# Four conv row blocks of an output projection as two pairs by Strassen's algorithm, with one written-out order for all engines, in a hybrid decoder layer

## The chip, the cores and the metric

The kernel runs on one core of a Trainium2 chip. The metric is the device time of one execution in microseconds; several executions are taken, and their median is given. Two kernels are compared on the same chip.

In the profile PE is the tensor engine, PEld its weight loads, DVE the vector engine, ACT the scalar engine, POOL the engine called GpSimd, and SP the engine that only issues transfers here. A row of a timeline reads: start, duration, engine, line, operation, output <- inputs, shape, count, and in brackets the idle time before it with what ended that.

## The reference

One layer with a conditioned mixer and a conditioned convolutional feed-forward part, for 512 tokens of 1024 channels. `ada_w` gives six modulation vectors from the condition `c`. What the change touches is the product with `w_out`, whose 2048 rows are 1024 of the mLSTM heads (`h`) and 1024 of the convolution group (`y`), and what follows it:

```python
mod = cond @ ada_w[l] + ada_b[l]
sh1, sc1, g1, sh2, sc2, g2 = jnp.split(mod[:, None, :], N_MOD, axis=-1)
...
mix = jnp.concatenate([h, y], axis=-1) @ w_out[l]
x = x + g1 * rms_norm(mix, mix_post_g[l])
u = rms_norm(x, ffn_pre_g[l]) * (1.0 + sc2) + sh2
up = causal_dwconv(u @ ffn_up[l], ffn_conv_w[l], ffn_conv_b[l])
```

All of it is float32.

## The kernel before

Every float32 product is made of three: each operand is split into a high part, rounded to the type `fp32r`, and a low part, the rest (`w_split` at L164 for weights, on ACT and POOL), and `mm3` (L186) issues high times high, high times low and low times high into one bank of PSUM, 128x512 float32.

The 512 tokens are four token tiles of 128. The 2048 rows of `w_out` are 16 blocks of 128, 0 to 7 from the heads and 8 to 15 from the convolution; `MIX` is the order in which they are used. The 1024 output columns are two halves of 512. `mixa` is the first half, four banks, one for each token tile; `mixb` is the second. `mix_first(n)` (L812 to L833) adds row block `MIX[n]` to the four banks of `mixa` with 12 matmuls. It stands between the steps of the last head's attention (`steps`), so that TensorE has work while the head's softmax and normalisation run. Then eight row blocks go into `mixb` (L847 to L851), all four token tiles after one another, and `mix_last(tt, a, b)` (L902) adds the other eight for one token tile at a time, so that a tile's row is whole early. `wo_rows` loads four row blocks of a half, 1 MB, by SP's queue into one of two buffers (`raws`) and splits them.

The modulation vectors are made beside this, by 48 sums, each of 1024 products for 128 outputs (`ada_block`, L147): a transfer of 0.5 MB by ACT's queue, then one VectorE instruction that multiplies and sums, L155. Sums 16 to 23 give `g1`; 24 to 39 give `sh2` and `sc2`. The latter were put behind the head's last split (`last_lo`). `ada_done` adds the bias, L160, and L852 to L854 turn the result into `gains`, which TensorE transposes (`gT` of 16 rows, L643, in `send_rows`); the rows go through DRAM (`row_d`) and come back spread over all partitions as `gs2r` and `sh2r` (`row`, L653). In the same way `gT` of 8 rows gives `g1r`.

For each token tile a chain follows when its `mixa` and `mixb` banks are whole: `sq_sum` on ACT (L668, `mixa0junk`, `mixb0junk`) sums the squares, `chain_sums` makes `un = mixb * g1r` and the factor `rm` (two small steps, DVE and POOL), `chain_x` the new `x1` and its sum of squares, with `gs2r`, `chain_u` the normalised input `un` with `sh2r`. TensorE transposes it (`xT`, L892), ACT and DVE split it (`u2h`, `u2l`), and `up`, the feed-forward product, begins. `mg` (L844) is `mixa * g1r`, made for four tiles while `mixb` is computed. `up_split` splits the second and third block of `w_up`, loaded by SP (L909).

What sets the order: on each engine instructions run in the order in which they were recorded and then scheduled by a planner that goes by priority; `with in_order()` keeps the recorded order for what stands in it, and `behind` pins one instruction after another of the same engine. Each engine's queue is in order, so an instruction that waits holds up all behind it. The queues of SP and ACT also issue transfers.

## Time and profile before

| | us |
|---|---|
| median of three runs | 773.16 |
| lowest and highest | 772.98, 774.11 |
| the profiled execution | 772.58 |
| its span in the profile | 770.9 |
| TensorE busy in it | 757.8 |
| VectorE busy | 606.3 |
| ScalarE busy | 403.9 |
| POOL busy | 350.9 |

The span is from the first to the last instruction in the profile; the execution's own time is 1.7 us longer. The mean granted TensorE clock was 0.997 of full speed.

The last head's attention and the first half of the projection lie at about 316 to 370 us, the first eight blocks of the second half at 370 to 392, the rest of it to 415, and from there `up` runs.

### The profile page before, as it was taken

To read this page: it belongs to the slowest core of one execution; us is meant where nothing else is said; L and a number is where in the kernel's file an instruction comes from. 1 tells how busy PE (TensorE), PEld (TensorE's weight loads), DVE (VectorE), ACT (ScalarE), POOL (GpSimd) and SP (SyncE) were. 2 spreads that over 40 slices of the span, in tenths; PEclk is the share of its full clock that TensorE was granted. 3 is DMA by queue.
4 is the path that set the end of the run, shared out by engine and by line. 5 is a ranking of instruction groups with operands and counts; after the bars stand their busy time and mean duration, and the time that the engine had idled before them with its cause. 6 is when DMAs were issued, how large, how long until landed. Compare 5 with 4: busy or idle time off the path is not lost.

```text
span 770.9 us, 10631 instructions
## 1 busy us (share of the span) xinstructions
PE 757.8 (98%) x3709; PEld 637.3 (83%) x3709; DVE 606.3 (79%) x967; ACT 403.9 (52%) x761; POOL 350.9 (46%) x286
## 2 busy tenths in 40 slices
PE   7999999999999999999999999999999999999996
PEld 5788898778888888988888998888888888878885
DVE  6987999999999856747758798666555687699996
ACT  5447256677676457572343554444444444455762
POOL 1029578697797645442751456444444440000001
PEclk9999999999999999999999999999999999999998
DMA  8983214204023552425953653333233321787872
GB/s 325 341 334 137 84 55 164 82 29 164 28 82 110 166 177 96 162 111 187 379 195 114 245 187 130 130 130 109 96 117 124 131 91 60 260 277 226 302 261 109
DMA packets 36409, 125.33 MB, mean 163 GB/s; under 512 B 4194, under 2 KB 5634, under 8 KB 30468
## 3 DMA queue, kind: packets, MB, share of 16 engines
q1 hardware_dynamic: 24372, 96.17, 35.5%
q10 hardware_dynamic: 11984, 28.48, 10.6%
q8 instruction: 29, 0.48, 0.2%
q14 instruction: 24, 0.20, 0.1%
HBM read 113.22 MB, written 11.42 MB: 162 GB/s over the span
## 4 chain that ended last, share of the span: by engine, by line
PE 90%; DVE 4%; DMA 2%; ACT 2%; issue 1%; POOL 0%; SPq 0%; DVEq 0%; ACTq 0%; POOLq 0%
PE up L190 10%; PE up L189 10%; PE up L188 10%; PE qko L188 6%; PE qko L189 5%; PE qko L190 5%; PE p L1175 5%; PE glu L189 3%; PE glu L188 3%; PE glu L190 3%; PE glu L316 2%; PE mixa L190 2%; PE mixa L188 2%; PE mixa L189 2%; PE mixb L188 2%; PE mixb L190 2%
## 5 line engine op out<-in xcount | busy, mean ns | idle before, releaser
L721 DVE SCALAR_TENSOR_TENSOR cv<-gt,cvw,cv 128x489 f32<-128x489 f32 (+23 forms) x200 | 136.9, 728 | 3.3 <-ACT cv L709 2.2
L675 POOL TENSOR_TENSOR ro2r<-ro2t,mhalf 128x1 f32<-128x1 f32 x1 | 0.5, 537 | 120.5 <-DVE ro2t L673 120.5
L171 POOL TENSOR_TENSOR wup_1024l<-wup,wup_1024h 128x512 fp32r<-128x512 f32 x20 | 27.5, 1373 | 31.7 <-ACT wup_1024h L170 31.6
L717 POOL TENSOR_TENSOR cs<-cs,cs 128x510 f32<-128x510 f32 (+3 forms) x32 | 41.3, 1291 | 0.2
L171 POOL TENSOR_TENSOR wup_0l<-wup,wup_0h 128x512 fp32r<-128x512 f32 x20 | 27.3, 1367 | 29.1 <-ACT wup_0h L170 29.1
L171 POOL TENSOR_TENSOR wup_1536l<-wup,wup_1536h 128x512 fp32r<-128x512 f32 x20 | 27.0, 1349 | 28.8 <-ACT wup_1536h L170 28.8
L155 DVE SCALAR_TENSOR_TENSOR junk<-ada,cb 128x1024 bf16<-128x1024 f32 x20 | 31.1, 1554 | 7.8 <-DMA ada<-in_adaT 7.7
L189 PE MATMUL up<-u2l,wup_0h 128*128 128x512 f32 (+1 forms) x100 | 36.5, 365 | 0.2 <-DVE u2l L900 0.2
L188 PE MATMUL up<-u2h,wup_0h 128*128 128x512 f32 (+1 forms) x100 | 36.5, 365 | 0.0
L188 PE MATMUL up<-u2h,wup_1024h 128*128 128x512 f32 (+1 forms) x100 | 36.4, 364 | 0.0
L190 PE MATMUL up<-u2h,wup_0l 128*128 128x512 f32 (+1 forms) x100 | 36.4, 364 | 0.0
L188 PE MATMUL up<-u2h,wup_512h 128*128 128x512 f32 (+1 forms) x100 | 36.4, 364 | 0.0
L189 PE MATMUL up<-u2l,wup_512h 128*128 128x512 f32 (+1 forms) x100 | 36.4, 364 | 0.0
L190 PE MATMUL up<-u2h,wup_512l 128*128 128x512 f32 (+1 forms) x100 | 36.4, 364 | 0.0
L188 PE MATMUL up<-u2h,wup_1536h 128*128 128x512 f32 (+1 forms) x100 | 36.4, 364 | 0.0
L189 PE MATMUL up<-u2l,wup_1536h 128*128 128x512 f32 (+1 forms) x100 | 36.4, 364 | 0.0
L190 PE MATMUL up<-u2h,wup_1536l 128*128 128x512 f32 (+1 forms) x100 | 36.4, 364 | 0.0
L190 PE MATMUL up<-u2h,wup_1024l 128*128 128x512 f32 (+1 forms) x100 | 36.4, 364 | 0.0
L189 PE MATMUL up<-u2l,wup_1024h 128*128 128x512 f32 (+1 forms) x100 | 36.3, 363 | 0.0
L171 POOL TENSOR_TENSOR wup_512l<-wup,wup_512h 128x512 fp32r<-128x512 f32 x20 | 27.7, 1383 | 14.9 <-ACT wup_512h L170 14.9
L715 ACT ACTIVATE cs<-gt,cvw 128x511 f32<-128x511 f32 (+4 forms) x40 | 27.4, 715 | 8.1 <-POOL cs L717 3.6
L170 ACT ACTIVATE wup_1024h<-wup 128x512 fp32r<-128x512 f32 x22 | 13.9, 631 | 25.1 <-PE up L189 21.4
(1070 smaller groups left out, 2663.6 us busy)
## 6 DMA issues: line engine op xcount, KB each, us to landing
wup<-in_w_up SPq DMA_DIRECT2D x22, 1024.0 KB, 6.6
wqko<-in_w_qko SPq DMA_DIRECT2D x12, 1024.0 KB, 4.8
ada<-in_adaT ACTq DMA_DIRECT2D x20, 512.0 KB, 4.3
ada<-in_adaT SPq DMA_DIRECT2D x16, 512.0 KB, 7.4
wo<-in_w_out SPq DMA_DIRECT2D x8, 1024.0 KB, 4.8
spare<-in_adaT ACTq DMA_DIRECT2D x12, 512.0 KB, 7.6
wd<-in_w_down SPq DMA_DIRECT2D x6, 768.0 KB, 6.5
g2kept<-g2d SPq DMA_DIRECT2D x11, 384.0 KB, 7.3
```

The lines of the kernel that those rows point to most:

```text
L155: t = V.scalar_tensor_tensor(out=junk, in0=r, scalar=1.0, in1=cb, op0=ALU.mult, op1=ALU.mult, accum_out=mod[:, i : i + 1])
L170: S.activation(hi[:, :n], src, AF.Copy)
L171: (eng or G).tensor_tensor(out=lo[:, :n], in0=src, in1=hi[:, :n].bitcast(F32), op=ALU.subtract)
L188: PE.matmul(ps, a[0], b[0], start=start, stop=False)
L189: PE.matmul(ps, a[0], b[1], start=False, stop=False)
L190: PE.matmul(ps, a[1], b[0], start=False, stop=stop)
L316: PE.matmul(banks0[i], blk(wk, i)[a], u[k][b], start=k == 0 and a == b, stop=False)
L675: G.tensor_tensor(out=r, in0=t, in1=mhalf[:, :1], op=ALU.pow)
L715: S.activation(t[:, d:], cvx[j][:, : T - d], AF.Copy, scale=w(CK - 1 - d))
L717: G.tensor_tensor(out=side[:, d:], in0=side[:, d:], in1=t[:, d:], op=ALU.add)
L721: last_tap[0] = V.scalar_tensor_tensor(out=cp[:, d:], in0=cvx[j][:, : T - d], scalar=w(CK - 1 - d), in1=cp[:, d:], op0=ALU.mult, op1=ALU.add)
L1175: PE.matmul(ps[q], x, y, start=False, stop=m == NM - 1 and i == 2, skip_group_check=True)
```

## The change

It takes the four convolution blocks 12 to 15 out of `MIX` and computes them as two pairs (12, 13) and (14, 15) by Strassen's algorithm: the two-by-two blocks are the two token halves (256 tokens), the two row blocks of the pair, and the two column halves. Seven products, p1 to p7, of two token tiles each take the place of eight; each is 6 matmuls for one pair, and the two pairs add up in the same banks. Strassen's sums over the tokens are made by `token_sums`, those over the weights by `row_sums` and `row_last`, in place in the loaded weights `wo_raw` (2 MB in the freed buffer of `u`, a new input `w_os` in which the host has set the four quarters of each pair side by side). `row_part` splits the weight sums with the low part on VectorE. The products use the banks of `mixa` and `mixb`: p1, p6, p7 in the banks of `mixb` 2 and 3, p5, p3 in 0 and 1, p2 in `mixa` 0 and 1, p4 in 2 and 3. Where a product belongs in several of the outputs, ACT copies the bank out (`op1`, `op5`, `ou`, `op7`) and VectorE adds the copy onto the other banks.

Half `mixb` now gets four row blocks for all tiles (`KA` = 4) and eight by `mix_last`. All of it stands in one `in_order()` block, for all engines. The loads of `x1` move from ACT's queue to SP's, behind the loads of `w_out`; the row `g1r` is sent and fetched by SP. Eleven of the sums 24 to 39 move up: 24 to 28 between the last head's projections, 29 to 34 ahead of the scaling of `hn`; 35 follows the splits for p4, 36 the first additions onto `mixa`, and 37 to 39 the last. Two small vectors, `cvw` and `ghalf`, are pinned behind the last split of `u`.

```diff
-MIX = [*range(6), *range(8, 14), 6, 7, 14, 15]
+MIX = [*range(6), *range(8, 12), 6, 7]
+PAIRS = [(12, 13), (14, 15)]
...
-    KA = 8
+    HT = T // 2
+    KF = 12
+    KA = 4
...
+    def token_sums(za, zb, name):
+        sums, s4 = cvtile(f"os{name}"), cvtile(f"o4{name}")
+        s1, s2 = sums[:, :HT], sums[:, HT:]
+        V.tensor_tensor(out=s1, in0=za[:, HT:], in1=zb[:, HT:], op=ALU.add)
+        V.tensor_tensor(out=za[:, HT:], in0=za[:, :HT], in1=za[:, HT:], op=ALU.subtract)
+        V.tensor_tensor(out=s2, in0=s1, in1=za[:, :HT], op=ALU.subtract)
+        V.tensor_tensor(out=s4[:, :HT], in0=zb[:, :HT], in1=s2, op=ALU.subtract)
+        return {"a": za, "b": zb, "s": sums, "4": s4[:, :HT]}
+    def token_part(z, kinds, name):
+        at = lambda z, h: [tuple(v[:, h * HT + q * P : h * HT + (q + 1) * P] for v in z) for q in range(2)]
+        out = {}
+        for n in kinds:
+            if n == "4":
+                t = slot(f"o4{name}t", F32R)
+                out["p3"] = at(pair(z[n], t[:, :HT], t[:, HT:]), 0)
+            else:
+                t = pair(z[n], slot(f"oh{name}{n}", F32R), slot(f"ol{name}{n}", F32R))
+                for h, which in enumerate({"a": ("p1", "p7"), "b": ("p2", "p4"), "s": ("p5", "p6")}[n]):
+                    out[which] = at(t, h)
+        return out
+    def row_part(which, m):
+        b = {"p1": 1, "p2": 0, "p6": 1, "p7": 2, "p3": 3, "p4": 0}.get(which)
+        z = ot1[m] if which == "p5" else wraw[m][:, b * T : (b + 1) * T]
+        wf[which, m] = w_split(z, f"o{which}_{m}", eng=V)
+    def row_sums(m):
+        b21, b11, b12, b22 = (wraw[m][:, b * T : (b + 1) * T] for b in range(4))
+        V.tensor_tensor(out=b12, in0=b22, in1=b12, op=ALU.subtract)
+        V.tensor_tensor(out=b11, in0=b11, in1=b12, op=ALU.add)
+    def row_last(m):
+        b21, b11 = (wraw[m][:, b * T : (b + 1) * T] for b in range(2))
+        V.tensor_tensor(out=b21, in0=b21, in1=b11, op=ALU.subtract)
+    def block(which, m):
+        ps = {"p1": banks[2:], "p6": banks[2:], "p7": banks[2:], "p5": banks[:2], "p3": banks[:2], "p2": mixa[:2], "p4": mixa[2:]}[which]
+        for q in range(2):
+            mm3(ps[q], tf[m][which][q], wf[which, m], m == 0 and which in ("p1", "p5"), m == 1, True)
...
+            if j >= KT // 2:
+                continue
...
+            tc.cur_priority += LATER
+            for i in range(16, 24):
+                ada_block(i, last_tap[0])
+            for i in range(24, 29):
+                ada_block(i, taps[H - 1, 1 if i < 27 else 3], acts[H - 1, 0 if i < 27 else 2])
+            tc.cur_priority -= LATER
...
         if h == H - 2:
             norm_sums()
-    tc.cur_priority += LATER
-    for i in range(16, 24):
-        ada_block(i, last_tap[0])
     ada_done(16, 24)
-    tc.cur_priority -= LATER
     gain(0, 16, "mix_post_g")
-    wo = {}
+    wo, tf, wf = {}, {}, {}
     steps = attention(H - 1)
     next(steps)
     mix_first(0)
+    wraw = upool.tile([P, 2, 2048], F32, tag="uh", name="wo_raw")
+    wraw = [wraw[:, m, :] for m in range(2)]
     next(steps)
     norm_rows()
-    mix_first(1)
-    mix_first(2)
-    mix_first(3)
-    mix_first(4)
+    za = token_sums(ys[4], ys[5], "0")
+    tf[0] = token_part(za, "asb4", "0")
+    spare.append(upool.tile([P, KT, T], F32, tag="ul", name="spare"))
+    for n in range(1, 5):
+        mix_first(n)
+    for m, r in enumerate(wraw):
+        nc.sync.dma_start(r, w_os[m])
+    rows0 = turn_rows(0, KT, cvbank)
     next(steps)
     mix_first(5)
     next(steps)
     mix_first(6)
-    next(steps)
-    for n in range(7, 10):
-        mix_first(n)
-    for _ in steps:
-        pass
-    spare.append(upool.tile([P, KT, T], F32, tag="ul", name="spare"))
-    for i in range(24, 40):
-        ada_block(i, last_lo[0])
+    mid = wo_rows(0, 8, 10)
+    ot1 = []
+    for m in range(2):
+        ot1.append(cvtile(f"ot1_{m}"))
+        V.tensor_tensor(out=ot1[m], in0=wraw[m][:, 2 * T : 3 * T], in1=wraw[m][:, T : 2 * T], op=ALU.subtract)
+    for i in range(29, 35):
+        ada_block(i, last_pair[0])
+    zb = token_sums(ys[6], ys[7], "1")
+    with in_order():
+        next(steps)
+        mix_first(7)
+        wo[0] = mid
+        for n in range(8, 10):
+            mix_first(n)
+        r10 = raws.tile([P, 2048], F32, tag="raw", name="wo10")
+        nc.sync.dma_start(r10[:, : 2 * T], w_out[0, :, 10 * T :])
+        send_turned(0, KT, rows0, nc.sync)
+        wide1 = vpool.tile([P, 2 * T + 8], F32, tag="vh", name="g1r")
+        g1r = row(0, lambda n: [wide1[:, :T], wide1[:, T : 2 * T]], "g1", nc.sync)
+        tf[1] = token_part(zb, "a", "1")
+        for which in ("p1", "p5"):
+            for m in range(2):
+                row_part(which, m)
+            if which == "p1":
+                tf[1].update(token_part(zb, "s", "1"))
+        wo[0] = [None, None] + [w_split(r10[:, n * T : (n + 1) * T], f"wo10_{n}", eng=V) for n in range(2)]
+        for i in range(35, 40):
+            ada_load(i)
+        for _ in steps:
+            pass
+        banks = [atbank(f"mixb{tt}") if tt < 2 else cvbank(f"mixb{tt}") for tt in range(NT)]
+        for which in ("p1", "p5"):
+            for m in range(2):
+                block(which, m)
+        for n in range(10, KF):
+            mix_first(n)
+        tf[1].update(token_part(zb, "b", "1"))
+        tf[1].update(token_part(zb, "4", "1"))
+        op1, op5 = ([cvtile(f"{n}_{q}") for q in range(2)] for n in ("op1", "op5"))
+        for m in range(2):
+            row_part("p2", m)
+        for q in range(2):
+            S.activation(op1[q], banks[2 + q], AF.Copy)
+        for m in range(2):
+            block("p2", m)
+        for m in range(2):
+            row_sums(m)
+        for q in range(2):
+            S.activation(op5[q], banks[q], AF.Copy)
+        for m in range(2):
+            row_part("p6", m)
+            block("p6", m)
+        for m in range(2):
+            row_last(m)
+        for m in range(2):
+            row_part("p4", m)
+            block("p4", m)
+        ada_op(35, last_lo[0])
+        for m in range(2):
+            row_part("p7", m)
+        for m in range(2):
+            row_part("p3", m)
+        wo_r = raws.tile([P, 2048], F32, tag="raw", name="wo1_0")
+        nc.sync.dma_start(wo_r, w_out[1, :, : 4 * T])
+        ou = vpool.tile([P, 2 * T + 8], F32, tag="vh", name="ou")
+        ou = [ou[:, q * T : (q + 1) * T] for q in range(2)]
+        for q in range(2):
+            S.activation(ou[q], banks[2 + q], AF.Copy)
+        for m in range(2):
+            block("p7", m)
+        for q in range(2):
+            V.tensor_tensor(out=banks[q], in0=banks[q], in1=ou[q], op=ALU.add)
+        for m in range(2):
+            block("p3", m)
+        mg = [slot(f"mg{tt}") for tt in range(NT)]
+        wo = [w_split(wo_r[:, n * T : (n + 1) * T], f"wo1_{n}") for n in range(2)]
+        for tt in range(2):
+            V.tensor_tensor(out=mixa[tt], in0=mixa[tt], in1=op1[tt], op=ALU.add)
+        ada_op(36, last_lo[0])
+        op7 = [cvtile(f"op7_{q}") for q in range(2)]
+        for q in range(2):
+            S.activation(op7[q], banks[2 + q], AF.Copy)
+        for q in range(2):
+            V.tensor_tensor(out=banks[2 + q], in0=banks[2 + q], in1=op5[q], op=ALU.add)
+        wo += [w_split(wo_r[:, n * T : (n + 1) * T], f"wo1_{n}") for n in range(2, 4)]
+        for q in range(2):
+            V.tensor_tensor(out=mixa[2 + q], in0=mixa[2 + q], in1=op7[q], op=ALU.add)
+        for i in range(37, 40):
+            ada_op(i, last_lo[0])
+        for tt in range(NT):
+            V.tensor_tensor(out=mg[tt], in0=mixa[tt], in1=g1r[0], op=ALU.mult)
+            sq_sum(mixa[tt], msq[:, 2 * tt : 2 * tt + 1], f"mixa{tt}")
     ada_done(24, 40)
-    for n in range(10, 2 * KT):
-        mix_first(n)
-        if n == 10:
-            send_rows(0, KT)
...
     for n_, k in enumerate(MIX[:KA]):
-        if n_ % 4 == 0:
-            wo = wo_rows(1, n_ // 4)
         for tt, ps in enumerate(banks):
-            mm3(ps, (hy[k][0][:, tok(tt)], hy[k][1][:, tok(tt)]), wo[n_ % 4], n_ == 0, False)
+            mm3(ps, (hy[k][0][:, tok(tt)], hy[k][1][:, tok(tt)]), wo[n_], False, False, True)
     V.scalar_tensor_tensor(out=gains[:, KT : 2 * KT], in0=sc2[:, :, 0], scalar=1.0, in1=vcols("ffn_pre_g", 0, KT), op0=ALU.add, op1=ALU.mult)
     V.tensor_scalar(out=gains[:, KT : 2 * KT], in0=gains[:, KT : 2 * KT], scalar1=RD, scalar2=None, op0=ALU.mult)
     V.tensor_copy(gains[:, 2 * KT : 3 * KT], sc2[:, :, 1])
-    wo = [w for g in range(KA // 4, 4) for w in wo_rows(1, g)]
-    HT = T // 2
+    wo = [w for a in range(KA, KF, 4) for w in wo_rows(1, a, a + 4)]
+    x1 = [[slot(f"x1_{tt}_{hf}") for hf in range(2)] for tt in range(NT)]
+    for tt in range(NT):
+        for hf in range(2):
+            nc.sync.dma_start(x1[tt][hf], x[tok(tt), hf * T : (hf + 1) * T])
+
     u2h = upool.tile([P, 2, KT, HT], F32R, tag="uh", name="u2h")
     u2l = upool.tile([P, 2, KT, HT], F32R, tag="ul", name="u2l")
```

On VectorE, after the first half of the projection: these rows are those around `mg` and `gains` before (`junk_31` is sum 31 and so on).

```order
L155 SCALAR_TENSOR_TENSOR junk_33_3583,mod_137<-spare_3552,cb_112 128x1024
L844 TENSOR_TENSOR mg0_3701<-mixa0_1372,g1r_3713 128x512
L844 TENSOR_TENSOR mg1_3702<-mixa1_1373,g1r_3713 128x512
L844 TENSOR_TENSOR mg2_3703<-mixa2_1374,g1r_3713 128x512
L844 TENSOR_TENSOR mg3_3704<-mixa3_1375,g1r_3713 128x512
L155 SCALAR_TENSOR_TENSOR junk_34_3587,mod_137<-ada_34_3585,cb_112 128x1024
L155 SCALAR_TENSOR_TENSOR junk_35_3591,mod_137<-ada_35_3589,cb_112 128x1024
L155 SCALAR_TENSOR_TENSOR junk_36_3594,mod_137<-spare_3552,cb_112 128x1024
L155 SCALAR_TENSOR_TENSOR junk_37_3597,mod_137<-spare_3552,cb_112 128x1024
L155 SCALAR_TENSOR_TENSOR junk_38_3600,mod_137<-spare_3552,cb_112 128x1024
L155 SCALAR_TENSOR_TENSOR junk_39_3603,mod_137<-spare_3552,cb_112 128x1024
L160 TENSOR_TENSOR mod_137<-mod_137,vec_111 128x16
```

And the same place now, with the additions of the copied banks:

```order
L997 TENSOR_TENSOR mixb3_3654<-mixb3_3654,op5_1_3713 128x512
L1000 TENSOR_TENSOR mixa2_1374<-mixa2_1374,op7_0_3849 128x512
L1000 TENSOR_TENSOR mixa3_1375<-mixa3_1375,op7_1_3850 128x512
L174 SCALAR_TENSOR_TENSOR junk_37_3865,mod_137<-spare_3351,cb_112 128x1024
L174 SCALAR_TENSOR_TENSOR junk_38_3867,mod_137<-spare_3351,cb_112 128x1024
L174 SCALAR_TENSOR_TENSOR junk_39_3869,mod_137<-ada_39_3629,cb_112 128x1024
L1004 TENSOR_TENSOR mg0_3833<-mixa0_1372,g1r_3590 128x512
L1004 TENSOR_TENSOR mg1_3834<-mixa1_1373,g1r_3590 128x512
L1004 TENSOR_TENSOR mg2_3835<-mixa2_1374,g1r_3590 128x512
L1004 TENSOR_TENSOR mg3_3836<-mixa3_1375,g1r_3590 128x512
L179 TENSOR_TENSOR mod_137<-mod_137,vec_111 128x16
L1010 SCALAR_TENSOR_TENSOR gains_1358<-mod_137,vec_111 128x8
```

Six sums stood between `mg` and `mod` before; now three stand ahead of `mg`, behind the additions, two of which take the copy of p7's banks, and `mod` follows `mg`.

On ACT, around the last sums of squares of `mixa` up to the first of `mixb` (`wo1_8` is the last load of four row blocks of the second half, `wup1` the second block of `w_up`), before:

```order
L170 ACTIVATE wo1_3_1536h_3907<-wo1_3_3893 128x512
L668 ACTIVATE mixa0junk_3725,msq_1371<-mixa0_1372 128x512
L668 ACTIVATE mixa1junk_3728,msq_1371<-mixa1_1373 128x512
L170 ACTIVATE wup0_0h_3915<-wup0_3913 128x512
L668 ACTIVATE mixa2junk_3731,msq_1371<-mixa2_1374 128x512
L170 ACTIVATE wup0_512h_3919<-wup0_3913 128x512
L668 ACTIVATE mixa3junk_3734,msq_1371<-mixa3_1375 128x512
L170 ACTIVATE wup0_1024h_3923<-wup0_3913 128x512
L170 ACTIVATE wup0_1536h_3927<-wup0_3913 128x512
L170 ACTIVATE wup1_0h_4025<-wup1_3931 128x512
L668 ACTIVATE mixb0junk_4029,msq_1371<-mixb0_3736 128x512
```

And now:

```order
L189 ACTIVATE wo1_8_0h_3955<-wo1_8_3953 128x512
L704 ACTIVATE mixa2junk_3878,msq_1371<-mixa2_1374 128x512
L189 ACTIVATE wo1_8_512h_3959<-wo1_8_3953 128x512
L704 ACTIVATE mixa3junk_3881,msq_1371<-mixa3_1375 128x512
L189 ACTIVATE wo1_8_1024h_3963<-wo1_8_3953 128x512
L189 ACTIVATE wo1_8_1536h_3967<-wo1_8_3953 128x512
L189 ACTIVATE wup0_0h_3991<-wup0_3989 128x512
L189 ACTIVATE wup0_512h_3995<-wup0_3989 128x512
L189 ACTIVATE wup0_1024h_3999<-wup0_3989 128x512
L189 ACTIVATE wup0_1536h_4003<-wup0_3989 128x512
L189 ACTIVATE wup1_0h_4101<-wup1_4007 128x512
L704 ACTIVATE mixb0junk_4105,msq_1371<-mixb0_3651 128x512
```

The splits of the last four row blocks of `w_out` stood ahead of the `mixa` sums of squares; now they stand between these, and the splits of `wup0` follow. In both, the first split of `wup1` stands directly ahead of `mixb0junk`.

More of the change, by code (lines that the diff above doesn't have):

```diff
@@ L170, in w_split @@
         S.activation(hi[:, :n], src, AF.Copy)
-        (eng or G).tensor_tensor(out=lo[:, :n], in0=src, in1=hi[:, :n].bitcast(F32), op=ALU.subtract)
+        op = (eng or G).tensor_tensor(out=lo[:, :n], in0=src, in1=hi[:, :n].bitcast(F32), op=ALU.subtract)
+        if pin is not None:
+            behind(op, pin)
         return hi, lo
@@ L184, in blk, with mm3 @@
         return hi[:, a : a + P], lo[:, a : a + P]
[L186 to L190 removed]
+    def mm3(ps, a, b, start, stop, onto=False):
+        for n, (x, y) in enumerate(((a[0], b[0]), (a[0], b[1]), (a[1], b[0]))):
+            PE.matmul(ps, x, y, start=start and n == 0, stop=stop and n == 2, skip_group_check=onto)
     def colsum(acc, n, name):
@@ L371, in decoder_layer, with behind @@
         glu_ps[i // 2, i % 2] = ps
+    def behind(op, other):
+        tc.add_manual_dep(op.ins, other.ins.name, mybir.DependencyInfo(mybir.DependencyClass.NoSync, mybir.DependencyReason.DATA),
+                          reason="order on VectorE")
     cvx = [None] * KT
@@ L439, in make_v, with pair @@
                 yield
-    def pair(z, hi, lo):
+    def pair(z, hi, lo, pin=None):
         S.activation(hi, z, AF.Copy)
-        V.tensor_tensor(out=lo, in0=z, in1=hi.bitcast(F32), op=ALU.subtract)
+        last_pair[0] = V.tensor_tensor(out=lo, in0=z, in1=hi.bitcast(F32), op=ALU.subtract)
+        if pin is not None:
+            behind(last_pair[0], pin)
         return hi, lo
+    last_pair = [None]
     def conv4(ps, i, name):
@@ L838, in decoder_layer @@
-    wide1 = vpool.tile([P, 2 * T + 8], F32, tag="vh", name="g1r")
-    g1r = row(0, lambda n: [wide1[:, :T], wide1[:, T : 2 * T]], "g1")
-    for tt in range(NT):
-        for hf in range(2):
-            nc.scalar.dma_start(x1[tt][hf], x[tok(tt), hf * T : (hf + 1) * T])
-    for tt, ps in enumerate(mixa):
-        V.tensor_tensor(out=mg[tt], in0=ps, in1=g1r[0], op=ALU.mult)
-        sq_sum(ps, msq[:, 2 * tt : 2 * tt + 1], f"mixa{tt}")
-    banks = [atbank(f"mixb{tt}") if tt < 2 else cvbank(f"mixb{tt}") for tt in range(NT)]
+    mid = wo_rows(0, 8, 10)
@@ L1293, in _layout @@
     wo = f("w_out")[0]
+    wo_ = wo.reshape(2 * KT, P, 2, T)
     return {
```

76 lines of the change are left out of this document (45 added, 31 removed).

## The prediction

> **What bounds the kernel now.** I read the busy shares first, then the chain that ended last, then the table of TensorE's waits, and last the timelines around the output projection. These are the busy line, the first line of the chain of waits, and the table of waits:
>
> ```profile
> PE 757.8 (98%) x3709; PEld 637.3 (83%) x3709; DVE 606.3 (79%) x967; ACT 403.9 (52%) x761; POOL 350.9 (46%) x286
> PE 90%; DVE 4%; DMA 2%; ACT 2%; issue 1%; POOL 0%; SPq 0%; DVEq 0%; ACTq 0%; POOLq 0%
> PE cps L139 <- DMA crow<-in_c: 2.3, 1, 2.3
> PE glu L316 <- ACT uh L336: 1.9, 1, 1.9
> PE xT L242 <- DVE dg L240: 1.2, 1, 1.2
> PE up L189 <- DVE u2l L900: 0.2, 1, 0.2
> ```
>
> TensorE works 98% of the span and carries 90% of the last chain. Its three longest waits, in the table above, belong to the first stage; the only one in the projection is 0.2 us at the head of `up`. The rows below are the busy times by stretch (columns: sum of busy time and count per engine, granted clock, DMA share, GB/s): the end of the projection's first half with half of the second, then the rest up to `up`.
>
> ```profile
> 352.40:391.60 39.20, 39.20 (x180) 32.36 (x178) 32.16 (x45) 13.61 (x27) 23.52 (x15) 1.00 0.78 284
> 391.60:415.70 24.10, 23.95 (x115) 19.75 (x113) 14.76 (x28) 8.58 (x21) 7.12 (x8) 1.00 0.48 173
> ```
>
> TensorE is busy for all of the first 39.20 us and for 23.95 of the next 24.10, at full granted clock. So here the time is TensorE's work; whatever leaves its queue is gained, unless another engine is then late. VectorE, at 32.16 of 39.20 us, is the one with the least room.
>
> **The change, part by part. First, the matmuls.** One block of K rows on one column half takes 4 token tiles times 3 matmuls. The starts of two neighbouring blocks:
>
> ```profile
> 369.80 0.39 PE L188 MATMUL mixb<-wo_0h,hh 128*128 128x512 f32 x1
> 372.52 0.39 PE L188 MATMUL mixb<-wo_512h,hh 128*128 128x512 f32 x1
> 391.56 0.27 PE L643 MATMUL gT<-ident,gains 128*16 128x128 f32 x1
> ```
>
> 372.52 − 369.80 = 2.72 us for 12 matmuls, 0.2267 us each. The four conv blocks were 4 × 2 × 12 = 96 matmuls; as two pairs of seven products, each of two token tiles times 3, they are 2 × 7 × 6 = 84. Twelve fewer, of the same shape: **−2.72 us**. By this the second transpose `gT`, which stood at 391.56, can come at 388.84, behind 48 matmuls of `mixb` (10.88 us), so that product p3 ends at 377.96 and p7, 12 matmuls ahead, at 375.24.
>
> **Second, what the products need.** Their sums and splits are about 50 instructions for VectorE and a few copies for ScalarE; POOL loses ten splits. TensorE runs nine other blocks over them, and by my walk through the order each product's operands are there 1.4 us (p7) to 4.7 us (p2) early, with the durations below. I cost them at nothing; the cover is thinnest at p7, whose banks must first be copied out.
>
> ```profile
> L1157 ACT ACTIVATE sp<-p 128x512 f32<-128x512 f32 x2 | 1.2, 588 | 0.3 <-PE p L190 0.3
> 719.95 0.69 DVE L1163 TENSOR_TENSOR p<-p,su 128x512 f32<-128x512 f32 x1
> 720.55 0.68 DVE L1004 TENSOR_TENSOR g2l<-g2kept,g2h 128x512 fp32r<-128x512 f32 x1
> ```
>
> The down projection already uses such a scheme: a bank is copied out in 0.588 us, and an addition onto a bank holds VectorE for 0.60 us (start to next start).
>
> **Third, the chain behind p7, on which my sum turns.** Before, the four `mg` products and the second modulation vector's sums ended long before `gT` had to read `gains`. The timelines of VectorE and of POOL there:
>
> ```profile
> 372.46 2.47 DVE L844 TENSOR_TENSOR mg<-mixa,g1r 128x512 f32<-128x512 f32 x4
> 374.86 1.21 DVE L155 SCALAR_TENSOR_TENSOR junk<-ada,cb 128x1024 bf16<-128x1024 f32 x1
> 378.46 2.07 DVE L155 SCALAR_TENSOR_TENSOR junk<-spare,cb 128x1024 bf16<-128x1024 f32 x1 [0.15 <-DMA spare<-in_adaT]
> 384.39 2.19 DVE L155 SCALAR_TENSOR_TENSOR junk<-spare,cb 128x1024 bf16<-128x1024 f32 x1
> 386.62 1.14 DVE L160 TENSOR_TENSOR mod<-mod,vec 128x16 f32<-128x16 f32 x1
> 387.80 1.21 DVE L852 SCALAR_TENSOR_TENSOR gains<-mod,vec 128x8 f32<-128x8 f32 x1
> 388.92 0.16 DVE L854 COPY gains<-mod 128x8 f32<-128x8 f32 x1
> 389.04 1.23 DVE L853 TENSOR_SCALAR gains<-gains 128x8 f32<-128x8 f32 x1
> 373.64 1.29 POOL L171 TENSOR_TENSOR wo_0l<-wo,wo_0h 128x512 fp32r<-128x512 f32 x1
> 377.18 2.27 POOL L171 TENSOR_TENSOR wo_1024l<-wo,wo_1024h 128x512 fp32r<-128x512 f32 x1
> 388.94 1.30 POOL L171 TENSOR_TENSOR wo_1536l<-wo,wo_1536h 128x512 fp32r<-128x512 f32 x1
> L657 DVE SCALAR_TENSOR_TENSOR gains<-mod,vec x2: 150/158/167, 275.7 to 468.3; 128x8 f32<-128x8 f32 x2
> ```
>
> A sum takes 1.21 us by itself and 2.07 to 2.19 beside a POOL split, and the split 1.29 or 2.27: they take turns, one of each in about 2.25 us. The same `gains` operation takes 0.158 us elsewhere (median, L657) and 1.21 here, one POOL split's length. So before, `gains` was ready at 389.04 + 1.23 = 390.27, with 1.29 us to spare.
>
> Now in VectorE's order the last sums (37 to 39) and `mg` stand behind the additions onto `mixa`, and two of those take the copy of p7's banks. p7 ends at 375.24; two copies, 1.2, to 376.5; the additions onto `mixb` and `mixa`, of which three follow the last copy, 1.8, to 378.4 with the handovers; three sums, 3.7 alone to 6.7 at 2.25 each; `mg` 2.47; `mod` and three `gains` steps 0.6 alone to 3.65 as in the rows (386.62 to 390.27). `gains` is ready between 385.2 and 391.2. POOL has twelve `wo` splits and four `wup` splits there, hardly a pause, so I stand near the upper end: 390.4. TensorE asks at 388.84 and its queue is in order, the rest of `mixb` behind `gT`: **+1.55 us** of stall (bounds 0 and 2.4). Eleven sums moved up cost nothing: VectorE idles 36.40 − 19.68 = 16.7 us in the stretch before.
>
> ```profile
> 316.00:352.40 36.40, 36.40 (x191) 31.33 (x191) 19.68 (x32) 23.46 (x49) 19.30 (x17) 1.00 0.40 145
> ```
>
> On the trading of turns the Trainium skill (page "SBUF — State Buffer", section "Who interferes with whom") says that VectorE and GpSimd contend for one port pair when the VectorE instruction has two SBUF inputs, not when it has at most one outside the two-port modes. The trace agrees: sums stretched, while `mg`, one input in PSUM, kept 0.62 us each beside a POOL split. By the rule `mg` and the additions onto banks stay short, as in the sum above.
>
> **Fourth, the loads and what follows.** The x loads now sit on SP's queue ahead of the `wup` loads, and the last `wo` block of four is loaded when POOL has split the fourth block before it. Rows of the second `wup` load, of ScalarE behind it, of the chain's last steps and of TensorE:
>
> ```profile
> 390.26 0.33 SPq L909 DMA_DIRECT2D wup<-in_w_up  x1
> 395.08 0.63 ACT L170 ACTIVATE wup_0h<-wup 128x512 fp32r<-128x512 f32 x1 [3.77 <-DMA wup<-in_w_up]
> 397.41 0.60 ACT L668 ACTIVATE mixb0junk<-mixb 128x512 bf16<-128x512 f32 x1 [1.70 <-PE mixb L190]
> 410.06 1.42 DVE L884 SCALAR_TENSOR_TENSOR un<-un,rf1r,sh2r 128x512 f32<-128x512 f32 x2 [0.66 <-POOL rf1r L675]
> 413.71 1.03 PE L892 MATMUL xT<-ident,un 128*128 128x128 f32 x8
> 415.72 0.39 PE L189 MATMUL up<-u2l,wup_0h 128*128 128x256 f32 x1 [0.17 <-DVE u2l L900]
> ```
>
> The load took 395.08 − 390.26 = 4.8 us. Before, the chain for token tile 1 ended at 410.06 + 1.42 = 411.48 and TensorE came for it at 413.71, 2.2 us later. Now the fourth block of the last four is split on ScalarE after `mixa1junk`, which follows `mg`: the four POOL splits run from about 387.7 to 392.9 (4 × 1.29), the second `wup` load starts then and lands at 397.7, and `mixb0junk`, next on ScalarE behind `wup_0h` (0.63), comes at 398.4 instead of 397.41. The chain ends at 412.5; TensorE comes 2.72 − 1.55 = 1.17 earlier, at 412.54. That is a tie; I take **+0.1** (bounds 0 and 1.5, the latter if the load takes the 6.6 us that is the median of `wup` loads).
>
> ```profile
> wup<-in_w_up SPq DMA_DIRECT2D x22, 1024.0 KB, 6.6
> ```
>
> **Sum.** −2.72 + 1.55 + 0.1 = −1.07 us. The profiled execution took 772.58 us (span 770.9, so 1.7 around it), and would come to 771.5. It lies 0.58 below the median of the runs, 773.16; the median comes to **772.1**. From here on 0.2%, 1.55 us, is about what a measurement of this kernel can tell from no change: faster is below 771.61, slower above 774.71.
>
> **Rivals.** *All of it arrives.* If POOL is done with its splits or waits for ScalarE while the three sums and `gains` run, these take 3.7 and 0.6 and `gains` is ready at 385.2, ahead of 388.84. For it: POOL lost ten splits, and in the rows it let one sum at 374.86 through in 1.21. Against: 388.94 and its like, POOL busy to the end. 773.16 − 2.72 = 770.4.
>
> *The work is out, and nothing comes of it.* `gains` at 391.2 (stall 2.4) and a load of 6.6 us (1.5): 773.16 − 2.72 + 2.4 + 0.3 to 1.5, 773.1 to 774.3. For it: VectorE's 32.16 of 39.20. Against: VectorE did part of its work earlier.
>
> *Slower, by POOL's last four `wo` splits.* SP's queue is in order: the second `wup` load waits for the last of these splits, and behind it stand the rows `gs2` and `sh2`. If the four take 2.27 each instead of 1.29, they end at 387.7 + 9.1 = 396.8 instead of 392.9, and everything on SP behind them is 3.9 us later. The chain for tile 1 then ends at 412.5 + 3.9 = 416.4, against TensorE's 412.54: a stall of 3.9, so 773.16 − 1.17 + 3.9 = 775.9. It eats the gain from a delay of about 1.2 us, and shows as slower from 2.8. Against it: VectorE has only four small steps left there, and POOL took 1.30 beside these (388.94). For it: SP also has eight x loads, 2 MB, to pass in that time, which at 284 GB/s are 7.4 us of transfer just ahead of `wup`; a load late by as much has the same effect.
>
> *The twelve matmuls do not leave the path,* because a product starves early: then a product's wait, not `gT`, appears in TensorE's table. p7's 1.4 us is the smallest cover; I put this with the slower case.
>
> **How the numbers follow.** The forecast (771.4 to 773.0) gets 0.40, the full gain 0.22, nothing 0.12, slower 0.26. Below 771.61 lie the full gain and a third of the forecast's case, 0.36; above 774.71 the slower case and a little of the third, 0.27; between, 0.37. For eight in ten I need the full gain and about half of the slower case: 770.3 to 775.6. The forecast's own range is 771.4 to 773.0.
>
> **What would show it.** 12 fewer matmuls, at 0.2267 us; a wait of TensorE for `gains` at `gT` of 1 to 2 us in its table; the three last sums at about 2.2 us each next to POOL splits; `mixb0junk` about 1 us behind its time before; no wait of TensorE between `hT` and `gT` for an operand of a product. I am wrong if `gT` waits for nothing (the full gain) or if a wait of more than 2 us stands at `xT` or `up` (the slower case), or if TensorE waits at p1 to p7.

## The result and the profile after

The changed kernel takes 776.13 us (median of seven runs, 775.01 to 778.46) against 773.14 us (772.61 to 774.89) for the kernel before beside it: a ratio of 1.0038, 95% interval 1.0025 to 1.0051. It is slower by about 3 us. The profiled execution took 775.74 us, with a span of 773.8 us, 2.9 us longer than before. Ratios below are likewise to the kernel before on the same chip, with the interval in brackets.

The page's busy line and the first line of the chain of waits, of the changed kernel:

```profile
PE 756.4 (98%) x3697; PEld 635.1 (82%) x3697; DVE 631.6 (82%) x1011; ACT 412.1 (53%) x779; POOL 339.1 (44%) x276
PE 78%; DVE 11%; ACT 3%; POOL 3%; issue 2%; DMA 2%; ACTq 0%; DVEq 0%; POOLq 0%; SPq 0%
```

TensorE has twelve matmuls fewer (3697 against 3709) and is busy 1.4 us less, but its share of the last chain fell from 90% to 78%, and VectorE's rose from 4% to 11%. What TensorE waited for, of the changed kernel (total us, times, longest us):

```profile
PE cps L140 <- DMA crow<-in_c: 2.4, 1, 2.4
PE glu L336 <- ACT uh L356: 1.9, 1, 1.9
PE xT L1053 <- DVE u2l L1061: 1.8, 1, 1.8
PE xT L262 <- DVE dg L260: 1.3, 1, 1.3
PE s L210 <- DVE ry_t L229: 1.1, 1, 1.1
PE mixb L210 <- DVE so L577: 0.8, 1, 0.8
PE xT L1053 <- DVE un L1045: 0.8, 1, 0.8
PE xT L1053 <- DVE un L1030: 0.6, 1, 0.6
```

Five of the eight are new: `s` (the last head's scores), `mixb` (product p5), and three at the transposes `xT` of the first two token tiles, 5.1 us in all. `gT`, where the prediction had its stall, is not in the table.

Two stretches show where the time went. The first goes from the taps of `q_1`, before anything that the change delays, to the 16-row `gT`; the second from there to the first matmul of `up`. The busy time by stretch, first of the kernel before:

```profile
281.85:391.56 109.71, 109.71 (x567) 93.79 (x566) 73.80 (x112) 58.43 (x127) 56.90 (x44) 1.00 0.49 178
391.56:415.27 23.71, 23.71 (x114) 19.79 (x113) 14.33 (x27) 8.42 (x21) 7.16 (x8) 1.00 0.49 176
```

and of the changed kernel (the same columns: length, TensorE, weight loads, VectorE, ScalarE, POOL):

```profile
281.50:391.10 109.60, 107.68 (x555) 91.56 (x554) 95.38 (x157) 64.13 (x141) 38.80 (x30) 1.00 0.48 170
391.10:418.80 27.70, 24.50 (x114) 19.59 (x113) 15.77 (x27) 10.70 (x26) 12.34 (x12) 1.00 0.59 206
```

The first stretch lost twelve matmuls (567 to 555) and 2.0 us of TensorE's work, but TensorE stood idle for 109.60 − 107.68 = 1.9 us, the waits at `s` and `mixb`; the stretch is as long as before. The second has the same 114 matmuls and is 4.0 us longer, 3.2 of it idle. So the gain was given back ahead of `gT`, and the loss came behind it. How large the loss is differs between executions: in four profiles below that leave the second stretch as it is (so_first, no_early_sums, asked_late, and after_again, which is the changed kernel once more) it lasts 25.9 to 26.8 us, and the waits at `xT` sum to 1.6 to 2.3 us instead of 3.2.

**The wait at `s`.** ScalarE's timeline of the changed kernel at the last head's splits:

```profile
296.80 1.60 ACTq L157 DMA_DIRECT2D ada<-in_adaT  x2
298.45 0.60 ACT L512 ACTIVATE so<-qko 128x512 f32<-128x512 f32 x1 [1.64 <-DVE junk L174]
298.95 0.62 ACT L466 ACTIVATE qkh<-q_0c 128x512 fp32r<-128x512 f32 x1
```

Two transfers for later sums are issued on ScalarE's queue; the buffer of one is still read by a sum on VectorE (`junk`), and `so` and the splits `qkh`, which VectorE and TensorE wait for, stand behind them.

**The wait at p5.** VectorE's timeline of the changed kernel behind the transposes `hT`:

```profile
356.15 0.68 DVE L577 SCALAR_TENSOR_TENSOR so<-so,hT 128x512 f32<-128x512 f32 x1
357.62 0.75 DVE L581 SCALAR_TENSOR_TENSOR hl<-so,ghalf,hh 128x512 fp32r<-128x512 f32 x1 [0.79 <-ACT hh L580]
358.29 0.68 DVE L577 SCALAR_TENSOR_TENSOR so<-so,hT 128x512 f32<-128x512 f32 x1
```

In the written-out order the second `so` stands behind the first `hl`, which waits 0.79 us for ScalarE. p5 writes the banks that `hT` used, so it waits for the second `so`. Before, the planner had put both `so` ahead.

**The waits at `xT`.** The four queues of the changed kernel, SP, ScalarE, POOL and VectorE in turn:

```profile
389.57 0.33 SPq L199 DMA_DIRECT2D wup<-in_w_up  x1
394.58 0.33 SPq L1070 DMA_DIRECT2D wup<-in_w_up  x1
396.63 0.63 ACT L189 ACTIVATE wup_0h<-wup 128x512 fp32r<-128x512 f32 x1 [5.47 <-DMA wup<-in_w_up]
399.39 0.63 ACT L189 ACTIVATE wup_0h<-wup 128x512 fp32r<-128x512 f32 x1 [0.56 <-DMA wup<-in_w_up]
399.93 0.58 ACT L704 ACTIVATE mixb0junk<-mixb 128x512 bf16<-128x512 f32 x1
393.26 1.29 POOL L190 TENSOR_TENSOR wo_1536l<-wo,wo_1536h 128x512 fp32r<-128x512 f32 x1
401.09 1.75 POOL L190 TENSOR_TENSOR wup_1536l<-wup,wup_1536h 128x512 fp32r<-128x512 f32 x1
402.79 1.00 POOL L711 TENSOR_TENSOR rm0r<-rm0t,mhalf 128x1 f32<-128x1 f32 x1
414.97 1.41 DVE L1045 SCALAR_TENSOR_TENSOR un<-un,rf1r,sh2r 128x512 f32<-128x512 f32 x2 [0.66 <-POOL rf1r L711]
416.30 1.28 DVE L1061 TENSOR_TENSOR u2l<-xT,u2h 128x512 fp32r<-128x512 f32 x2
```

POOL ended the last split of `w_out` at 393.26 + 1.29 = 394.55, and SP issued the second `wup` load at 394.58, 4.3 us later than before. ScalarE had `mixb0junk` behind that load's first split, at 399.93 against 397.41. On POOL `rm0r` stood behind the four splits of the first `wup` load, which had been issued at 389.57 and landed only at 396.6; before, it was issued at 381.71, and its last split ended 3.8 us ahead of `rm0r`, as POOL's timeline of the kernel before shows:

```profile
393.94 1.30 POOL L171 TENSOR_TENSOR wup_1536l<-wup,wup_1536h 128x512 fp32r<-128x512 f32 x1
399.03 0.93 POOL L675 TENSOR_TENSOR rm0r<-rm0t,mhalf 128x1 f32<-128x1 f32 x1 [3.79 <-DVE rm0t L673]
```

The chain of tile 1 ended 4.9 us later than before (414.97 against 410.06), and the second `xT` waited, beyond it, for `u2l`, which frees the two banks that it writes.

### The profile page after: what moved, and what is told of

Read it like the earlier page. It is cut to its first block, busy times and chain, and to the rows that moved or that the text cites. A ratio compares the mean times of both kernels' runs of the same rounds, so it can differ in the third digit from the quotient of the medians.

```text
span 773.8 us, 10661 instructions
## 1 busy us (share of the span) xinstructions
PE 756.4 (98%) x3697; PEld 635.1 (82%) x3697; DVE 631.6 (82%) x1011; ACT 412.1 (53%) x779; POOL 339.1 (44%) x276
## 4 chain that ended last, share of the span: by engine, by line
PE 78%; DVE 11%; ACT 3%; POOL 3%; issue 2%; DMA 2%; ACTq 0%; DVEq 0%; POOLq 0%; SPq 0%
PE up L210 31%; PE qko L210 13%; PE glu L210 8%; PE p L210 8%; PE p L1336 4%; PE v L210 3%; DVE cv L802 2%; PE glu L336 2%; PE mixa L210 2%; DVE junk L174 1%; PE mixb L210 1%; PE s L534 1%; PE o L553 1%; DMA wup<-in_w_up 1%; DVE hn L569 1%
## 5 line engine op out<-in xcount | busy, mean ns | idle before, releaser
L174 DVE SCALAR_TENSOR_TENSOR junk<-ada,cb 128x1024 bf16<-128x1024 f32 x24 | 38.0, 1584 | 7.3 <-DMA ada<-in_adaT 7.1
```

Of the source, the lines that this page charges most:

```text
L174: t = V.scalar_tensor_tensor(out=junk, in0=r, scalar=1.0, in1=cb, op0=ALU.mult, op1=ALU.mult, accum_out=mod[:, i : i + 1])
```

## The experiments

Ten kernels ran. The kernel before ran beside them, at medians of 772.98 to 773.59 us.

**so_first.** In the last head the two `so` products stand ahead of both splits.

```diff
         for e in range(2):
             ...
             V.scalar_tensor_tensor(out=t, in0=t, scalar=1.0, in1=tp, op0=ALU.add, op1=ALU.mult)
-            hi, lo = slot(f"hh{h}_{e}", F32R), slot(f"hl{h}_{e}", F32R)
+            last.append(hidden)
+        for f in last:
+            f()
```

> In the last head both so products stand ahead of both hidden splits on VectorE, so that the second bank of hT is read without waiting for ScalarE's hh. Theory: the 0.81 us that TensorE waited at the first product into mixb (p5) comes from this order; the wait goes, p7 ends about 0.8 us earlier, and with it POOL's splits, the loads and the chain for the token tiles: about 775.3 us against 776.1. Rival: the chain for the token tiles starts from a load that does not depend on p7; then the 0.8 us turn up again at xT, and the time stays 776.1.

774.77 us, ratio 1.0018 (0.9999 to 1.0038). The wait at `mixb` is gone from TensorE's table, and VectorE runs both `so` in one go. The theory holds for its place. Its waits at `xT`, 2.3 us, lie between the 3.2 of the changed kernel's profile and the 1.7 of after_again's, so whether the 0.8 us turn up again there, as the rival has it, is open; the size of the gain (0.8 expected; by medians 1.4 against the first runs of the changed kernel and 1.0 against its later ones) is not settled by so wide an interval.

**no_early_sums.** Without the sums 24 to 28.

```diff
-                ada_block(i, taps[H - 1, 1 if i < 27 else 3], acts[H - 1, 0 if i < 27 else 2])
+                ada_load(i, acts[H - 1, 0 if i < 27 else 2])
```

> Leaves out the five sums 24 to 28 (their columns are zero; their transfers stay), which stand among the last head's projections. Theory: they put VectorE 3.6 us behind there (hn at 304.49 against 300.88) and so cause TensorE's wait of 1.10 us at s; it goes, and about 1.1 us is gained, 775.0 us. Rival: what delays s is ScalarE or the bank of the row statistics, not VectorE; then the wait at s stays near 1.1 us and the time near 776.1.

774.04 us, ratio 1.0007 (0.9992 to 1.0022). The wait at `s` fell from 1.1 to 0.2 us; from the taps of `q_1` to `gT` it took 108.67 us (281.25 to 389.92) against 109.63. So the five early sums and what they hold up cost about 1 us there, as the theory has it. Without the sums the issues on ScalarE's queue take only 0.34 us each there, so this run does not tell VectorE's time from the queue's.

**chain_first and chain_free.** In both the first steps of tile 0's chain (`chain_sums` and `chain_x`) are written ahead of the splits of the second `wup` load; in chain_free the low parts of the first `wup` load are made on VectorE too, and `gTs` is sent ahead of them.

```diff
-        up_split(1, raw1, slots, "t")
         r = chain_sums(0)
-        up_split(1, raw1, slots, "t")
         r = chain_x(0, r)
+        up_split(1, raw1, slots, "t")
+        up_split(1, raw1, slots, "t")
         chain_u(0, r)
...
-    up_w = {0: w_load(w_up[0], "wup0", slots, "t")}
+    up_w = {0: w_load(w_up[0], "wup0", slots, "t", V)}
```

> The chain of token tile 0 is written ahead of the first two splits of wup1, so ScalarE and VectorE no longer wait for that load before mixb0junk; POOL is as it was. Theory (two waits that end together, wup1's load on ScalarE and wup0's four splits on POOL, which ended 402.84): POOL still holds rm0r to about 402.8, so the waits at xT fall by 0.5 us at most, about 775.7 us. Rival: the wup1 load alone is what is late; then mixb0junk comes near 398.4 instead of 399.93 and the waits at xT fall by 1.5 us or more, 774.5 us.

> As chain_first, and the low parts of wup0 are made on VectorE (idle from 391.7 to 400) instead of POOL, with gTs sent ahead of them. Theory (both waits): rm0r comes near 400 instead of 402.79; the waits at xT, 3.2 us, fall to about 1, limited then by the rows gs2 and sh2: about 773.9 us. Rival: the rows gs2 and sh2, sent behind the wup1 load, are what is late; then un from x and gs2r stays near 405 and the time near 776.

chain_first: 776.05 us, ratio 1.0033 (1.0015 to 1.0051), no gain: `mixb0junk` came at 397.40, 2.5 us earlier, but `rm0r` only 1.3 us earlier, at 401.53, POOL having ended the `wup` splits at 400.29 + 1.29. chain_free: 775.00 us, ratio 1.0022 (1.0005 to 1.0039); `rm0r` at 400.00, and the waits at `xT` 1.2 us, against 2.8 in chain_first, 3.2 in the changed kernel's profile and 1.7 in after_again's. So two waits ended close together, and with only one lifted the other held the chain. What it is worth in time is not settled: the intervals of chain_free and of the changed kernel overlap widely. What came next is in VectorE's timeline of chain_free:

```profile
403.31 0.69 DVE L1040 TENSOR_TENSOR un<-x,gs2r 128x512 f32<-128x512 f32 x1 [0.93 <-DMA gs2r<-row_d]
404.63 0.69 DVE L1040 TENSOR_TENSOR un<-x,gs2r 128x512 f32<-128x512 f32 x1 [0.63 <-DMA gs2r<-row_d]
```

the row `gs2`, whose way through DRAM SP starts behind the `wup` load: a third wait, 1.6 us, which the changed kernel's profile does not show: there the chain reached these two steps only at 405.16.

**turn_early.** Tile 0's transpose is read out of its banks in the gaps of tile 1's chain.

```diff
-        r = chain_x(1, r)
+        turn_hi(0)
+        r = chain_x(1, r, (lambda: turn_lo(0, 0), lambda: turn_lo(0, 1)))
         chain_u(1, r)
-        turn_out(0)
```

> Token tile 0 is read out of its transpose's banks (u2h, u2l) in the gaps of tile 1's chain, where it stood behind that chain. Theory: the second transpose xT waits for these banks, by 1.80 us in the changed kernel's table and 1.2 in three of its variants, so the prediction set the end of the chain 1.2 us too early; the wait named u2l goes, a wait for un of 0.5 us may take its place, and 1.0 to 1.3 us are gained: about 774.9 us against 776.1. Rival: the transpose waits for un itself, and u2l is only named because it ends last; then the wait stays above 1 us and the time is 776.

775.85 us, ratio 1.0022 (1.0009 to 1.0036). TensorE's table of turn_early has no wait for `u2l` any more:

```profile
PE xT L1056 <- DVE un L1030: 0.6, 1, 0.6
PE xT L1056 <- DVE un L1048: 0.5, 1, 0.5
```

The second `xT` now waits 0.5 us for `un` itself, as expected. The ratio is not clearly below the 1.0027 of after_again, so the wait is shown, its price not.

**asked_late.** The transfers for sums 29 to 34 are issued behind the last head's `qkh`.

```diff
     for i in range(29, 35):
-        ada_block(i, last_pair[0])
+        ada_block(i, last_pair[0], split_act)
```

> The transfers for the sums 29 to 34 are asked for behind the last head's splits qkh on ScalarE's queue; the sums stay where they are. Theory: it is not VectorE's time for the sums 24 to 28 but ScalarE's queue that made s late, its issue of two transfers at 296.80 having waited 1.60 us for a buffer that a sum still read, with so and qkh behind it; qkh comes near 297.4 instead of 298.95, TensorE's wait at s falls from 1.10 to 0.2 or less, about 775.1 us. Rival: the taps of k_2, put off by three sums on VectorE (288.71 against 286.11), make it late; then the wait at s stays above 0.7 and the time is 776.

773.75 us, ratio 1.0005 (0.9993 to 1.0017). `qkh` came 16.55 us behind the taps of `q_1` (281.57 to 298.12), 17.46 before the edit (281.49 to 298.95): 0.9 us earlier. But the wait at `s` was still 0.9 us, not 0.2, so the queue is not all of it. The time fell by more than the first stretch accounts for: that is only 0.2 us shorter in this profile (109.46 us), while the second, which the edit does not touch, is 1.8 us shorter (25.87). after_again, the changed kernel once more, shows that the hold of ScalarE's queue is not always the same:

```profile
296.62 2.84 ACTq L157 DMA_DIRECT2D ada<-in_adaT  x2
```

> The changed kernel once more, beside the two below on one chip. Both theories expect 776, a ratio of 1.0025 to 1.005, and waits at s, p5 and xT of about 1.1, 0.8 and 3 us; if it lies near 1.001 instead, part of what the single edits seemed to gain is the chip's.

It took 775.73 us, ratio 1.0027 (1.0013 to 1.0041), as expected, so the gains of combo2 and combo3, on the same chip, are not the chip's; its waits at `xT` were 1.7 us, not 3. In its profiled execution (777.32 us, the slowest of its nine) the same two issues held ScalarE for 2.84 us instead of 1.60: the sum whose buffer they needed waited 0.44 us for its own transfer and took 2.06 us instead of 1.23. They held it for 2.84 in the profile of so_first as well, that kernel's slowest execution (778.34 us). In both profiles TensorE then waited about 1.6 us in two steps instead of 1.1 in one, and right behind these waits its matmuls slowed down. TensorE's timeline of after_again:

```profile
316.64 1.05 PE L216 MATMUL ry_s<-ones,ysq 128*128 128x1 f32 x8 [1.00 <-DVE so L577]
320.33 0.69 PE L210 MATMUL s<-qkh,qkh 128*128 128x384 f32 x1 [0.64 <-DVE ry_t L229]
322.42 0.63 PE L210 MATMUL mixa<-wo_0h,hh 128*128 128x512 f32 x1
322.84 0.63 PE L210 MATMUL mixa<-wo_0l,hh 128*128 128x512 f32 x1
```

The last two start 0.42 us apart, where such matmuls elsewhere start 0.23 apart; the granted clock was 0.50 from 320 to 323 us and 0.60 from 323 to 326, against 1.00 in the first profile of the changed kernel. TensorE's busy time from the taps of `q_1` to `gT` was 110.9 us instead of 107.7, so these 3.2 us, and not the 1.2 us of the longer hold, are most of what that execution lost there. That the longer wait brings the clock down is not shown; the two stood together in both profiles. asked_late takes away the hold at this place, and none of its ten executions was slower than 775.5 us or had a mean clock below 0.997, while two of the sixteen of the changed kernel had 0.994 (777.32 and 778.46 us). So few cannot move the median: what brought it down in asked_late stays open, and the two intervals still touch.

**combo.** so_first, chain_free, turn_early and asked_late, the x loads ahead of the last `w_out` load, and the rows ahead of the second `wup` load.

```diff
-    wo = [w for a in range(KA, KF, 4) for w in wo_rows(1, a, a + 4)]
+    wo = wo_rows(1, 4, 8)
     x1 = [[slot(f"x1_{tt}_{hf}") for hf in range(2)] for tt in range(NT)]
     ...
+    wo += wo_rows(1, 8, 12)
...
-    raw1 = raw_up(1)
-    send_rows(KT, 2 * KT, nc.sync)
+    send_turned(KT, 2 * KT, rows1, nc.sync)
     gs2r = row(1, cvtile, "gs2", nc.sync)
     sh2r = row(2, cvtile, "sh2", nc.sync)
+    raw1 = raw_up(1)
```

> All of it together: so_first, chain_free, turn_early and asked_late, with the x loads ahead of the last load of w_out and the rows gs2 and sh2 ahead of the wup1 load. Theory (five separate waits, 1.1 at s, 0.8 at p5 and 3.2 at xT, each with its own cause): the waits between 316 and 420 us fall from 5.1 to about 1, and the twelve matmuls show: 771.5 to 772.2 us, 0.1 to 0.2% below the kernel before. Rival: what is taken from one engine is late on the next, since VectorE and POOL have no room in this stage; then waits of 2.5 us or more remain and the time is 773.5 or more.

772.32 us, ratio 0.9982 (0.9971 to 0.9993): faster than the changed kernel, and than the kernel before by 0.2%. Waits of 2.6 us remained between 316 and 420, as the rival has it and not the theory's 1, though the time lies only 0.1 us above the theory's. ScalarE and VectorE of combo show the largest:

```profile
402.86 0.63 ACT L189 ACTIVATE wup_0h<-wup 128x512 fp32r<-128x512 f32 x1 [3.36 <-DMA wup<-in_w_up]
404.74 1.41 DVE L1060 SCALAR_TENSOR_TENSOR un<-un,rf0r,sh2r 128x512 f32<-128x512 f32 x2
```

Tile 0's chain stood behind the splits of the second `wup` load, now asked for after the rows.

**combo2 and combo3.** In combo2 these splits stand behind the chain of tile 1; combo3 puts sum 26 behind the taps of `k_2` as well.

```diff
         chain_u(1, r)
+        up_split(1, raw1, slots, "t")
+        up_split(1, raw1, slots, "t")
         turn_tile(1)
...
-                ada_block(i, taps[H - 1, 1 if i < 27 else 3], acts[H - 1, 0 if i < 27 else 2])
+                ada_block(i, taps[H - 1, 1 if i < 26 else 2 if i < 27 else 3], acts[H - 1, 0 if i < 27 else 2])
```

> As combo, and the splits of wup1 stand behind the chain of token tile 1, so that no step of the chains waits for that load. Theory: in combo tile 0's chain stood from 399.5 to 404.74 behind these splits, whose load landed at 402.86, and this is what is left at xT (1.2 and 0.6 us); both go, 0.8 at s remains, about 771.0 us, 0.3% below the kernel before. Rival: tile 2's chain, which now has the splits, is late instead; then a wait of 1 us or more stands at the third xT and the time stays at 772.3.

> As combo2, and sum 26 stands behind the taps of k_2 instead of ahead of them. Theory: the sums ahead of k_2 put that head's splits, and so s, off by the 1.2 us that a sum takes; the wait at s falls from 0.8 to 0.2 or less, about 770.5 us. Rival: ScalarE's queue alone decides when s starts; then the wait at s stays at 0.8 and the time is that of combo2.

combo2: 771.82 us, ratio 0.9979 (0.9967 to 0.9990); combo3: 770.08 us, ratio 0.9950 (0.9934 to 0.9966). In combo2 no `xT` waits; tile 2 is not late, but `up` waits 1.1 us for `u2l` of tile 1, which now stands behind three of the moved splits. The expectation did not have this wait, and its time was 0.8 us too low. In combo3 the wait at `s` for `ry_t` is gone too (0.6 in combo2). The two stretches of combo3, cut at the same instructions as above:

```profile
283.92:391.12 107.20, 107.20 (x556) 91.71 (x556) 95.62 (x157) 63.97 (x141) 38.71 (x29) 1.00 0.51 178
391.12:414.81 23.69, 23.69 (x115) 19.79 (x113) 15.91 (x29) 10.82 (x26) 6.08 (x8) 1.00 0.60 219
```

TensorE is busy for all of both. The first is 109.71 − 107.20 = 2.5 us shorter than before, and the second has its old length. But the cut lies at the first matmul of `up`, and the wait at `up` falls directly behind it, in combo3 as in combo2. VectorE and TensorE of combo3:

```profile
414.84 0.68 DVE L190 TENSOR_TENSOR wup_1024l<-wup,wup_1024h 128x512 fp32r<-128x512 f32 x1
415.44 1.28 DVE L1076 TENSOR_TENSOR u2l<-xT,u2h 128x512 fp32r<-128x512 f32 x2
416.18 0.39 PE L210 MATMUL up<-u2l,wup_0h 128*128 128x256 f32 x1 [1.09 <-DVE u2l L1076]
```

Before, this wait was 0.17 us. Up to this matmul combo3 is 1.6 us shorter than the kernel before (283.92 to 416.18 against 281.85 to 415.72): of the twelve matmuls' 2.72 us that is what is left. Its median lies 3.1 us below that of the kernel before, about twice as much, and this profile cannot say where the rest is from: the profiled execution, 772.79 us, is the slowest of the six, and its span, 770.9 us, is no shorter than before, above all because the taps of `q_1` came 2.1 us later.

## Why the prediction was wrong

The forecast was 772.1 us with 0.36 for faster; the kernel is slower, at 776.13, 3.1 us above the forecast's own range (771.4 to 773.0) and 0.5 above the wider one (to 775.6). The likeliest case was wrong. The rival that ends on the other side (775.9) came within 0.2 us, by a chain that it had only in part: that it came so near is luck. Two of the signs named for being wrong came, no wait at `gT` and a wait at one of p1 to p7; the waits at `xT` sum to more than 2 us, though none alone does.

- **The matmuls** went as said: twelve fewer, and combo3 recovers 2.5 of the 2.72 us up to `gT`, 1.6 up to the wait at `up`.
- **"Eleven sums moved up cost nothing" is the first step that failed.** The idle time given for it, 16.7 us of VectorE, lay in the stretch 316 to 352, but five of the sums went to 283 to 298, among the last head's taps. There they held VectorE ahead of `k_2` and, by their buffers, ScalarE's queue ahead of `qkh`: 1.1 us at `s` in the profile, and about 1.6, in two waits, where the queue was held longer. no_early_sums, asked_late and combo3 each took part of it away.
- **"Each product's operands are there early: I cost them at nothing" was right for the operands and wrong for the banks.** p5 waited 0.8 us for the bank of `hT`, not for an operand. The written-out order has the second `so` behind the first `hl`, and the prediction did not follow it; in so_first, with the order turned, the wait is gone.
- **The stall of 1.55 us at `gT` did not come.** `gains` was ready at 389.60 + 1.22 = 390.82, near the 390.4 forecast, but only because p7 was late: it ended at 377.51 instead of 375.24, 1.9 of these 2.3 us being the waits at `s` and p5. TensorE was as late, and `gT` at 391.12 waited for nothing. The term was mis-sized: measured from the end of p7, `gains` took 13.3 us, where the forecast had 15.2. These rows of VectorE's timeline of the changed kernel show why:

```profile
380.20 1.22 DVE L174 SCALAR_TENSOR_TENSOR junk<-spare,cb 128x1024 bf16<-128x1024 f32 x1
381.46 2.19 DVE L174 SCALAR_TENSOR_TENSOR junk<-spare,cb 128x1024 bf16<-128x1024 f32 x1
383.69 2.19 DVE L174 SCALAR_TENSOR_TENSOR junk<-ada,cb 128x1024 bf16<-128x1024 f32 x1
388.21 0.16 DVE L179 TENSOR_TENSOR mod<-mod,vec 128x16 f32<-128x16 f32 x1
389.60 1.22 DVE L1011 TENSOR_SCALAR gains<-gains 128x8 f32<-128x8 f32 x1
391.42 0.28 DVE L678 COPY gTs<-gT 16x128 f32<-16x128 f32 x1 [0.60 <-PE gT L676]
```

The first of the three sums took 1.22 us, the other two 2.19, and `mod` 0.16 instead of 1.14; the upper end, near which the forecast stood, had 2.25 for each sum and 3.65 for the four small steps, which took 2.6. In combo p7 ended at 375.29 and TensorE came to `gT` at 388.89, both within 0.1 us of the prediction, and `gains` was ready at 387.54, 1.35 us ahead.
- **"+0.1" for the loads and what follows was the step that decided**: the second stretch grew by 4.0 us in the profiled execution, and by 2.2 to 3.1 in the four other profiles that leave it as it is. Its place was right (POOL's last splits of `w_out`, SP's `wup` load behind them, ScalarE's `mixb0junk` behind that), and three things in it were wrong. POOL ended at 394.55, not 392.9. `rm0r` on POOL stands behind four splits of the first `wup` load, issued 7.9 us later than before, which the sum did not have; chain_first shows that these alone were enough to hold the chain. And the end of tile 1's chain was set at `chain_u`, 2.2 us ahead of `xT`, though the transpose also needs the banks that `u2l` frees. In the changed kernel `xT` started at 417.04, just behind the first of the two `u2l` (416.30 + 0.68); before, that one ended at 411.40 + 0.68 = 412.08, so the slack was 1.6 us.

The rival of a slower kernel had the right queue, but its mechanism, POOL's four splits stretched to 2.27 us each, did not happen: all four took 1.29. They were late because they started late, at 389.51 instead of 387.7.

## What to carry to other kernels

When TensorE is busy 98% of the time, fewer matmuls bring all other engines forward against their own deadlines; before the saving is counted, each bank, buffer and queue behind which a product or a transpose stands has to be followed, not its operands alone. A transfer issued on a computing engine's queue is an instruction of that engine: if its buffer is not free, what stands behind it waits (here 1.60 us, and 2.84 in other executions). And where work is moved into idle time, the idle time must be that of the place it goes to, not of the stage next to it.

## What the runs showed of the hardware

The same two issues on ScalarE's queue held it for 1.60 us in one execution of the changed kernel and for 2.84 in another.

In the two profiles with the hold of 2.84 us (after_again and so_first) the granted clock fell to 0.5 for some us behind TensorE's wait, and its mean from the taps of `q_1` to `gT` was 0.97 instead of 1.00. TensorE's busy time there was 110.9 and 110.5 us instead of 107.7.

The first `wup` load, issued with the x loads just ahead of it, was there 7.1 us later in the changed kernel's profile (389.57 to 396.63, ScalarE's first split of it) and 6.3 to 7.2 us later in seven others with this order; with the x loads moved, in combo, combo2 and combo3, it took 4.8 to 4.9 us (387.34 to 392.20 in combo).
